# An encoder trunk in split fp32: the two parts of x pass the upper weights in one 512-column matmul, in separate PSUM banks

## The chip, the core and the metric

The kernel runs on one core of one Trainium2 chip. The metric is the time of one execution on the device in microseconds (us). The engines are named as in the profile: PE (matmul), PEld (loading of its stationary operand), ACT, DVE, POOL and SP, which issues the DMAs. Each engine works through its own instructions in program order and waits at semaphores for the others.

## What is computed

Two layers (DEPTH = 2) over 256 tokens of 1024 features, each of three parts: a feed-forward part (FFN), a part with three token mixers, and a second FFN. Every part ends in a layer norm.

```python
def swiglu(x, w_gate, w_up, w_down):
    return (jax.nn.silu(x @ w_gate) * (x @ w_up)) @ w_down
...
    for l in range(DEPTH):
        x = layer_norm(ALPHA * x + 0.5 * swiglu(x, ffn1_w_gate[l], ffn1_w_up[l], ffn1_w_down[l]),
                       ln_g[l, 0], ln_b[l, 0])
        proj = x @ w_in[l]
        u, gb, gc, h, q, k, v = jnp.split(proj, splits, axis=-1)
        y_a = pool_mixer(u, pool_w[l], pool_scale[l])
        y_b = gated_conv_mixer(gb, gc, h, conv_w[l])
        y_c = neighbourhood_attention(q, k, v, rpb[l])
        y = jnp.concatenate([y_a, y_b, y_c], axis=-1) @ w_out[l]
        x = layer_norm(ALPHA * x + y, ln_g[l, 1], ln_b[l, 1])
        x = layer_norm(ALPHA * x + 0.5 * swiglu(x, ffn2_w_gate[l], ffn2_w_up[l], ffn2_w_down[l]),
                       ln_g[l, 2], ln_b[l, 2])
```

The hidden width of an FFN is 2816 (22 chunks of 128). Attention has 8 heads of 64 features; a query sees all 4 grid rows and 16 of the 64 columns.

## The kernel before

**Numbers in two parts.** Every weight and every activation that meets a weight is kept as an upper part (`hi`, fp32r, an ACT cast) and a rest (`lo`, a DVE subtraction). A product is the sum of three: hi x hi, hi x lo, lo x hi; so every product is three matmuls.

**Weights.** 320 units of 128 x 1024 numbers (512 KB) come from memory in the order of `plan`. `load` (L182) issues the DMA on SP into `raw`, then the cast (L179) and the subtraction (L180). At most 12 units are live (`W_SLOTS` is 24 tiles); a unit's tiles are taken over when PE has read it for the last time.

**Order.** The schedule is written by hand. `Pacer` keeps a model clock: `step(us)` moves it on, runs the hooks that have come due (`at(delay, tag, fn)`) and emits the load of one more unit. `need(tag)` runs the hooks of a tag at once. So the order on every engine is that in which the program's lines run.

**Three kinds of product.** `x_stat` (L275, the first gate/up columns and v, u, gate of the mixers): x is stationary, the weights stream, 512 columns each. `w_stat` (L295): the weights are stationary, x streams, so that the result comes out transposed (features x tokens). One call computes 256 features for all 256 tokens: two halves (`ft`) of 128 features, 8 chunks of the contraction each, three matmuls of 256 columns per chunk; both halves lie in one PSUM bank of 512 columns. An FFN calls it for 9 pairs of hidden chunks, gate and up; a mixer part for q0, k0, q1, k1, gc and h. `r_stat` (L312): down and output projections, 512 columns, accumulated over all chunks in four banks (2 token halves x 2 feature halves).

**PSUM.** Eight banks in two pools of four: `mm` for everything that is soon read out, `acc` for the scores S of attention and for the four accumulators of `r_stat`. A new tile takes over the bank of the tile four allocations earlier in its pool, once that has been read out.

**Reading out.** A gate goes from its bank through ACT's silu (L392), an up by DVE with the gate (L397), then into hi and lo (L481, L482). q goes by ACT in mirrored pieces (L772), k and gc by ACT copies (L776, L788), h by a DVE product with gc (L794).

**The mixer part.** Its order after v, u and gate is: q0, k0, then attention of head group 0 by hooks while q1, k1 run; attention of group 1 while gc and h run. Attention is a chain: scores (L699, PE), bias and maximum (L708, L710, DVE), exponential (L713, ACT), normalisation (L723, L725, DVE), transposes (L734, PE), copies (L739, ACT), product with v (L748, PE), and its parts (L761 ACT, L762 DVE). The convolution (L675 to L681) follows h on DVE. Then comes the output projection (L804 on), over the chunks in the order 0, 1, 4, 5, 6, 7, 2, 3: the pool mixer's two chunks, attention's four, the convolution's two.

Of the kernel before, what the change touches and what calls it, by code (L numbers as in the profile page):

```python
# [63 lines left out]
MM256 = 0.1095  # L64
# [57 lines left out]
def encoder_kernel(  # L122
# [172 lines left out]
    def w_stat(ps, key, xT):  # L295

        for ft in range(2):
            c = slice(ft * P, (ft + 1) * P)
            for i in range(2):
                hi, lo = pc.get((*key, i))  # L300
                for j in range(4):
                    kc = i * 4 + j
                    o = ps[:, ft * SEQ : (ft + 1) * SEQ]
                    PE.matmul(o, hi[:, j, c], xT[0][:, kc, :], start=(kc == 0), stop=False)  # L304
                    PE.matmul(o, hi[:, j, c], xT[1][:, kc, :], start=False, stop=False)  # L305
                    PE.matmul(o, lo[:, j, c], xT[0][:, kc, :], start=False, stop=(kc == KC - 1))  # L306
# [93 lines left out]
    def ffn(key, xT, next_gb, stop, store=False):  # L400
        hts = {0: new_h(), 1: new_h()}

        def gated_transposed(t, gate, up):
            hf = gated(up, gate[0])

            def tr_():
                tr = bank().rearrange("p (a b) -> p a b", a=4)
                for j in range(4):
                    PE.transpose(tr[:, j, :], hf[:, j * P : (j + 1) * P], ident)
                ts = slice(t * P, (t + 1) * P)  # L410
                for q in range(2):
                    src = tr[:, 2 * q : 2 * q + 2, :]
                    ACT.copy(hts[q][:, 0, :, ts], src)
                    DVE.tensor_tensor(hts[q][:, 1, :, ts], src, f32(hts[q][:, 0, :, ts]), ALU.subtract)
# [55 lines left out]
        for p in range(2, NPAIR):  # L470
            if key[1] == 0 and p == 6:
                pc.at(0, "bias", bias_ahead)
            gate = bank()
            w_stat(gate, (*key, "g", p), xT)
            sg = silu(gate)
            pc.step(12 * MM256)
            up = bank()
            w_stat(up, (*key, "u", p), xT)
            hT = hts[p] = new_h()
            hf = gated(up, sg).rearrange("p (a b) -> p a b", a=2)  # L480
            ACT.copy(hT[:, 0], hf)  # L481
            DVE.tensor_tensor(hT[:, 1], hf, f32(hT[:, 0]), ALU.subtract)  # L482
            pc.step(12 * MM256)
            pc.need("h")

            for q in behind(p):
                for f in (2 * q, 2 * q + 1):
                    k = (*key, "d", f)
                    for t in range(NT):
                        for n in range(2):  # L490
                            if acc[t][n] is None:
                                acc[t][n] = bank("acc")
                            r_stat(acc[t][n], k, act(k), t, n, f == 0, False)
                        if t == 1:
# [103 lines left out]
    def mixers(l, xT, next_gb, stop):  # L598
# [11 lines left out]
        POOL.memset(U[:, :, PADL + SEQ :], 0.0)  # L610
        biases, rv1 = dict(ahead.pop("bias")), ahead.pop("rv")

        def pool_means():
# [15 lines left out]
            def product():  # L629
                ps = bank().rearrange("p (a b) -> p a b", a=2)  # L630
# [34 lines left out]

        def proj(name):
            ps = bank()
            w_stat(ps, (*key, name), xT)
            return ps.rearrange("p (a b) -> p a b", a=2)
# [13 lines left out]
        def attention(j, qT, kT, q):  # L683
# [59 lines left out]
            def weighted():  # L743
                po = bank()[:, 0:SEQ].rearrange("p (b r c) -> p b r c", b=2, r=ROWS)
# [21 lines left out]
        def qk(q):  # L766
            pq = proj(f"q{q}")
            qT = hp.tile([P, 2, 2, P], F32, tag="qk", bufs=4, name=nm("qT"))
            for j in range(2):
# [24 lines left out]
        DVE.tensor_tensor(z[:, :, 1 : SEQ + 1], p_, gc, ALU.mult)  # L794
# [64 lines left out]
```

## Time and profile before

| what | value |
|---|---|
| median of 3 runs | 964.16 us (964.05 to 966.96) |
| the profiled execution | 966.65 us, its span 964.9 us |
| granted PE clock, mean | 0.996 |
| weights' cast L179 / rest L180 | 321 each, 1045 / 1240 ns |
| 512-column matmuls, L316 to L318 and L291 to L293 | 3 x 416 and 3 x 192 |
| DMA | 178.95 MB, mean 185 GB/s |

The page's slices show how evenly PE is used (busy tenths in 40 slices, then the clock granted and the share of the DMA engines):

```profile
PE   7999999998999999999999999999999999999996
...
PEclk9999999999999999999999999999999999999998
DMA  8877685447543776565458766754664358666601
```

The first layer's mixer part lies at about 206 to 292 us of the span, the second's at 682 to 765 us; the rest but for the first 30 us are FFNs. A matmul's record begins when the one before is still in flight, so records overlap, and the pace of PE is read from the distance of two starts.

### The profile page before, as it was taken

The numbers are of one execution on the slowest core, as the hardware profiler recorded it, in microseconds if no ns is written. First come the engines' busy times: TensorE is split into PE (matmuls) and PEld (weight loads), VectorE is DVE, ScalarE is ACT, GpSimd is POOL, SyncE is SP. The second block draws the span as 40 slices with busy tenths as digits, with TensorE's granted clock in tenths as the row PEclk, the third lists the DMA queues.
The fourth block names the chain that finished last, engine by engine and source line by source line (L and its number), as shares of the span: only waits on it lengthen the run. The fifth ranks groups of instructions, "written<-read, shape, count | busy, mean of one in ns | idle before, by whom it ended". The sixth has DMA issues, their size and how long they took to land.

```text
span 964.9 us, 15250 instructions
## 1 busy us (share of the span) xinstructions
PE 946.9 (98%) x6201; PEld 861.3 (89%) x6201; DVE 572.1 (59%) x682; ACT 437.4 (45%) x585; POOL 58.6 (6%) x106
## 2 busy tenths in 40 slices
PE   7999999998999999999999999999999999999996
PEld 5999999988888999999888999998898889999995
DVE  5756364685678654544686445556766775454525
ACT  6545344344834544443354444444465454444420
POOL 4000100004100000000000001000050000000000
PEclk9999999999999999999999999999999999999998
DMA  8877685447543776565458766754664358666601
GB/s 285 286 238 248 162 244 181 145 150 218 158 131 132 242 238 189 182 197 175 131 176 257 222 189 172 223 178 145 193 216 126 122 188 273 182 179 189 190 23 43
DMA packets 129077, 178.95 MB, mean 185 GB/s; under 512 B 14752, under 2 KB 100848, under 8 KB 129008
## 3 DMA queue, kind: packets, MB, share of 16 engines
q1 hardware_dynamic: 129008, 177.99, 59.8%
q8 instruction: 48, 0.79, 0.3%
q14 instruction: 21, 0.17, 0.1%
HBM read 176.84 MB, written 1.13 MB: 184 GB/s over the span
## 4 chain that ended last, share of the span: by engine, by line
PE 89%; ACT 3%; DVE 3%; DMA 3%; issue 1%; SPq 0%; DVEq 0%; ACTq 0%
PE mm L304 15%; PE mm L305 15%; PE mm L306 15%; PE acc L316 10%; PE acc L317 10%; PE acc L318 10%; PE mm L293 4%; PE mm L291 4%; PE mm L292 4%; DVE wlo L180 2%; ACT whi L179 2%; ACT pz L713 1%; DMA raw<-in_w_in_dram 1%; PE mm L734 1%; DMA raw<-in_ffn_w_up_dram 1%; PE mm L269 1%
## 5 line engine op out<-in xcount | busy, mean ns | idle before, releaser
L180 DVE TENSOR_TENSOR wlo<-raw,whi 128x1024 fp32r<-128x1024 f32 (+1 forms) x321 | 392.2, 1240 | 302.6 <-ACT whi L179 299.3
L179 ACT CAST whi<-raw 128x1024 fp32r<-128x1024 f32 (+1 forms) x321 | 330.9, 1045 | 323.6 <-issue 111.0
L304 PE MATMUL mm<-xhi,whi 128*128 128x256 f32 x1344 | 382.3, 284 | 0.0
L305 PE MATMUL mm<-xlo,whi 128*128 128x256 f32 x1344 | 381.0, 283 | 0.0
L306 PE MATMUL mm<-xhi,wlo 128*128 128x256 f32 x1344 | 380.9, 283 | 0.0
L304 PEld LDWEIGHTS mm<-xhi,whi 128*128 128x128 f32 x1344 | 258.4, 192 | 2.8 <-issue 1.5
L305 PEld LDWEIGHTS mm<-xlo,whi 128*128 128x128 f32 x1344 | 258.5, 192 | 1.3
L306 PEld LDWEIGHTS mm<-xhi,wlo 128*128 128x128 f32 x1344 | 258.5, 192 | 0.0
L316 PE MATMUL acc<-whi,hT 128*128 128x512 f32 x352 | 137.9, 392 | 0.0
L317 PE MATMUL acc<-whi,hT 128*128 128x512 f32 x352 | 137.4, 390 | 0.0
L318 PE MATMUL acc<-wlo,hT 128*128 128x512 f32 x352 | 137.0, 389 | 0.0
L318 PEld LDWEIGHTS acc<-wlo,hT 128*128 128x128 f32 x352 | 66.1, 188 | 14.0
L316 PEld LDWEIGHTS acc<-whi,hT 128*128 128x128 f32 x352 | 66.2, 188 | 12.7
L317 PEld LDWEIGHTS acc<-whi,hT 128*128 128x128 f32 x352 | 66.2, 188 | 12.4
L291 PE MATMUL mm<-whi,xhi 128*128 128x512 f32 x192 | 77.0, 401 | 0.0
L293 PE MATMUL mm<-wlo,xhi 128*128 128x512 f32 x192 | 75.4, 393 | 0.2 <-DVE wlo L180 0.2
L292 PE MATMUL mm<-whi,xlo 128*128 128x512 f32 x192 | 75.4, 393 | 0.0
L481 ACT CAST hT<-hf 128x512 fp32r<-128x512 f32 x36 | 22.3, 620 | 75.2 <-DVE hf L397 75.2
L344 POOL TENSOR_TENSOR rs<-rs,half_t 128x1 f32<-128x1 f32 x12 | 11.7, 977 | 653.4 <-DVE rs L343 653.4
L293 PEld LDWEIGHTS mm<-wlo,xhi 128*128 128x128 f32 x192 | 36.3, 189 | 8.7 <-DVE wlo L180 1.1
L291 PEld LDWEIGHTS mm<-whi,xhi 128*128 128x128 f32 x192 | 36.4, 190 | 8.1 <-ACT whi L179 1.2
L292 PEld LDWEIGHTS mm<-whi,xlo 128*128 128x128 f32 x192 | 36.5, 190 | 7.1
(93 smaller groups left out, 535.9 us busy)
## 6 DMA issues: line engine op xcount, KB each, us to landing
raw<-in_ffn_w_up_dram SPq DMA_DIRECT2D x88, 512.0 KB, 4.8
raw<-in_ffn_w_down_dram SPq DMA_DIRECT2D x88, 512.0 KB, 4.2
raw<-in_ffn_w_gate_dram SPq DMA_DIRECT2D x87, 512.0 KB, 4.2
raw<-in_w_in_dram SPq DMA_DIRECT2D x40, 512.0 KB, 4.4
raw<-in_w_out_dram SPq DMA_DIRECT2D x16, 512.0 KB, 4.6
lng<-in_ln_g_dram SPq DMA_DIRECT2D x6, 512.0 KB, 4.8
lnb<-in_ln_b_dram SPq DMA_DIRECT2D x6, 512.0 KB, 6.1
rbias<-tab SPq DMA_DIRECT2D x16, 96.0 KB, 3.3
```

The source lines that it names most:

```text
L179: ACT.copy(hi, raw)
L180: DVE.tensor_tensor(lo, raw, f32(hi), ALU.subtract)
L291: PE.matmul(ps, xT[0][:, kc, ts], hi[:, j, :], start=(kc == 0), stop=False)
L292: PE.matmul(ps, xT[1][:, kc, ts], hi[:, j, :], start=False, stop=False)
L293: PE.matmul(ps, xT[0][:, kc, ts], lo[:, j, :], start=False, stop=(kc == KC - 1))
L304: PE.matmul(o, hi[:, j, c], xT[0][:, kc, :], start=(kc == 0), stop=False)
L305: PE.matmul(o, hi[:, j, c], xT[1][:, kc, :], start=False, stop=False)
L306: PE.matmul(o, lo[:, j, c], xT[0][:, kc, :], start=False, stop=(kc == KC - 1))
L316: PE.matmul(ps, act[0][:, ts], hi[:, n, :], start=first, stop=False)
L317: PE.matmul(ps, act[1][:, ts], hi[:, n, :], start=False, stop=False)
L318: PE.matmul(ps, act[0][:, ts], lo[:, n, :], start=False, stop=last)
L481: ACT.copy(hT[:, 0], hf)
```

## The change

1. x's two parts lie in one tile, per chunk of the contraction 256 columns of hi and 256 of lo side by side. In `w_stat` the stationary upper weights meet both parts in one matmul of 512 columns; the rest of the weights then meets the hi part, into the first 256 columns. Two matmuls per chunk take the place of three.
2. Each half of 128 features has a bank of its own. When a half is done, ACT copies columns 256 to 511 to SBUF (with the scale) and DVE adds columns 0 to 255. What followed (silu, product with the gate, mirrored copies of q, product with gc) reads the sum from SBUF, with one step more.
3. The banks of `mm` are thus used up twice as fast. The transposes of hidden chunks, the pool mixer's product, the transposes of the softmax, attention's product with v and the transposed constants take banks of `acc`.
4. All attention is emitted ahead of the output projection; `columns` (constants) moves from the first FFN to the first mixer part. The model clock counts 0.347 us per chunk.

```diff
     def new_xT():
-        hi = xp.tile([P, KC, SEQ], F32R, tag="xhi", name=nm("xhi"))
-        lo = xp.tile([P, KC, SEQ], F32R, tag="xlo", name=nm("xlo"))
-        return hi, lo
+        both = xp.tile([P, KC, 2, SEQ], F32R, tag="xT", name=nm("xT"))
+        return both[:, :, 0], both[:, :, 1], both.rearrange("p k i s -> p k (i s)")
...
-    def w_stat(ps, key, xT):
+    def w_stat(key, xT, out, scale=1.0):
+        ps = [bank() for _ in range(2)]
         for ft in range(2):
             c = slice(ft * P, (ft + 1) * P)
             for i in range(2):
                 hi, lo = pc.get((*key, i))
                 for j in range(4):
                     kc = i * 4 + j
-                    o = ps[:, ft * SEQ : (ft + 1) * SEQ]
-                    PE.matmul(o, hi[:, j, c], xT[0][:, kc, :], start=(kc == 0), stop=False)
-                    PE.matmul(o, hi[:, j, c], xT[1][:, kc, :], start=False, stop=False)
-                    PE.matmul(o, lo[:, j, c], xT[0][:, kc, :], start=False, stop=(kc == KC - 1))
+                    PE.matmul(
+                        ps[ft], hi[:, j, c], xT[2][:, kc], start=(kc == 0), stop=False, skip_group_check=True
+                    )
+                    PE.matmul(
+                        ps[ft][:, 0:SEQ], lo[:, j, c], xT[0][:, kc],
+                        start=False, stop=(kc == KC - 1), skip_group_check=True,
+                    )
                 if ft == 1:
                     pc.free((*key, i))
+                if i == 1:
+                    o = out[:, ft]
+                    ACT.activation(o, ps[ft][:, SEQ:], AF.Copy, scale=scale)
+                    DVE.scalar_tensor_tensor(o, ps[ft][:, 0:SEQ], scale, o, ALU.mult, ALU.add)
                 if ft == 0 or i == 0:
-                    pc.step(12 * MM256)
+                    pc.step(4 * MM768)
...
-            gate = bank()
-            w_stat(gate, (*key, "g", p), xT)
-            sg = silu(gate)
...
+            sg = tp.tile([P, 2, SEQ], F32, tag="t", name=nm("sg"))
+            w_stat((*key, "g", p), xT, sg)
+            ACT.activation(sg, sg, AF.Silu)
...
-            hf = gated(up, sg).rearrange("p (a b) -> p a b", a=2)
+            DVE.tensor_tensor(hf, hf, sg, ALU.mult)
...
-                    tr = bank().rearrange("p (a b) -> p a b", a=2)
+                    tr = bank("acc").rearrange("p (a b) -> p a b", a=2)
...
-                po = bank()[:, 0:SEQ].rearrange("p (b r c) -> p b r c", b=2, r=ROWS)
+                po = bank("acc")[:, 0:SEQ].rearrange("p (b r c) -> p b r c", b=2, r=ROWS)
...
-        DVE.tensor_tensor(z[:, :, 1 : SEQ + 1], p_, gc, ALU.mult)
+        DVE.tensor_tensor(z[:, :, 1 : SEQ + 1], h, gc, ALU.mult)
...
-        pc.need("ya")
-        pc.need("a0")
+        for tag in ("ya", "a0", "a1"):
+            pc.need(tag)
```

Two places in the order matter below. The first is PE at the end of the first layer's mixer part. Before, from the last product of attention (into the banks mm_2911, whose rows stand just ahead, and mm_2921) to the first matmuls of the output projection (four accumulators acc_...):

```order
L748 MATMUL mm_2921<-PT_2857,v_2101 64x256
L748 MATMUL mm_2921<-PT_2864,v_2101 64x256
L316 MATMUL acc_2936<-whi_2363,yT_2606 128x512
L317 MATMUL acc_2936<-whi_2363,yT_2606 128x512
L318 MATMUL acc_2936<-wlo_2364,yT_2606 128x512
L316 MATMUL acc_2940<-whi_2363,yT_2606 128x512
L317 MATMUL acc_2940<-whi_2363,yT_2606 128x512
L318 MATMUL acc_2940<-wlo_2364,yT_2606 128x512
L316 MATMUL acc_2944<-whi_2363,yT_2606 128x512
```

and now the same stretch (acc_2645 just ahead), with the semaphores for which a row waits in brackets:

```order
L753 MATMUL acc_2655<-PT_2597,v_1898 64x256
L753 MATMUL acc_2655<-PT_2604,v_1898 64x256
L324 MATMUL acc_2670<-whi_2155,yT_2360 128x512 [waits PE_49]
L325 MATMUL acc_2670<-whi_2155,yT_2360 128x512
L326 MATMUL acc_2670<-wlo_2156,yT_2360 128x512
L324 MATMUL acc_2674<-whi_2155,yT_2360 128x512 [waits PE_49]
L325 MATMUL acc_2674<-whi_2155,yT_2360 128x512
L326 MATMUL acc_2674<-wlo_2156,yT_2360 128x512
L324 MATMUL acc_2678<-whi_2155,yT_2360 128x512 [waits DVE_49,PE_49]
L325 MATMUL acc_2678<-whi_2155,yT_2360 128x512
L326 MATMUL acc_2678<-wlo_2156,yT_2360 128x512
L324 MATMUL acc_2682<-whi_2155,yT_2360 128x512 [waits DVE_49,PE_49]
```

The order of the matmuls is the same; the product with v is now in `acc`, and the third and fourth accumulators wait for DVE, which empties acc_2645 and acc_2655. On DVE those are the rows of L767, behind h's second half (L316), z and the convolution:

```order
L180 TENSOR_TENSOR wlo_2616<-raw_2614,whi_2615 128x1024
L316 SCALAR_TENSOR_TENSOR h_2557<-mm_2559,h_2557 128x256
L799 TENSOR_TENSOR z_2630<-h_2557,gc_2450 128x2x256
L680 TENSOR_SCALAR cs_2634<-z_2630,cw 128x256
L682 SCALAR_TENSOR_TENSOR cs_2634<-z_2630,cw,cs_2634 128x256 x2
L680 TENSOR_SCALAR cs_2634<-z_2630,cw 128x256
L682 SCALAR_TENSOR_TENSOR cs_2634<-z_2630,cw,cs_2634 128x256 x2
L683 TENSOR_TENSOR cs_2634<-cs_2634,GB_1900 128x512
L686 TENSOR_TENSOR yT_2642<-cs_2634,yT_2642 128x512
L767 TENSOR_TENSOR yT_2650<-acc_2645,yT_2650 128x4x32 x2
L767 TENSOR_TENSOR yT_2650<-acc_2655,yT_2650 128x4x32 x2
```

Before, DVE has the same rows there but for the one of L316. The second place is DVE ahead of the normalisation of head group 1 (reciprocal and scaling of the softmax). Before:

```order
L710 TENSOR_REDUCE mx_2742<-Sb_2740 128x2
L180 TENSOR_TENSOR wlo_2777<-raw_2775,whi_2776 128x1024
L723 RECIPROCAL sm_2717<-sm_2717 128x2
L725 TENSOR_SCALAR pz_592<-pz_592,sm_2717 128x4x40 x2
L723 RECIPROCAL sm_2724<-sm_2724 128x2
```

and now:

```order
L715 TENSOR_REDUCE mx_2496<-Sb_2494 128x2
L316 SCALAR_TENSOR_TENSOR gc_2450<-mm_2451,gc_2450 128x256
L180 TENSOR_TENSOR wlo_2525<-raw_2523,whi_2524 128x1024
L316 SCALAR_TENSOR_TENSOR gc_2450<-mm_2452,gc_2450 128x256
L728 RECIPROCAL sm_2471<-sm_2471 128x2
L730 TENSOR_SCALAR pz_564<-pz_564,sm_2471 128x4x40 x2
```

The evictions of gc's two halves now stand around the weight split (on ACT their copies stand around its cast in the same way); head group 0 has the halves of q1 there.

More of the change, by code (lines that the diff above doesn't have):

```diff
@@ L63 @@
 MM512 = 0.218
-MM256 = 0.1095
+MM768 = 0.347
 class Pacer:
@@ L406, in tr_ @@
             def tr_():
-                tr = bank().rearrange("p (a b) -> p a b", a=4)
+                tr = bank("acc").rearrange("p (a b) -> p a b", a=4)
                 for j in range(4):
@@ L472, in ffn @@
                 pc.at(0, "bias", bias_ahead)
-            gate = bank()
-            w_stat(gate, (*key, "g", p), xT)
-            sg = silu(gate)
-            pc.step(12 * MM256)
-            up = bank()
-            w_stat(up, (*key, "u", p), xT)
+            sg = tp.tile([P, 2, SEQ], F32, tag="t", name=nm("sg"))
+            w_stat((*key, "g", p), xT, sg)
+            ACT.activation(sg, sg, AF.Silu)
+            pc.step(4 * MM768)
+            hf = tp.tile([P, 2, SEQ], F32, tag="t", name=nm("hf"))
+            w_stat((*key, "u", p), xT, hf, 0.5)
             hT = hts[p] = new_h()
-            hf = gated(up, sg).rearrange("p (a b) -> p a b", a=2)
+            DVE.tensor_tensor(hf, hf, sg, ALU.mult)
             ACT.copy(hT[:, 0], hf)
             DVE.tensor_tensor(hT[:, 1], hf, f32(hT[:, 0]), ALU.subtract)
-            pc.step(12 * MM256)
+            pc.step(4 * MM768)
             pc.need("h")
@@ L546, in columns @@
         def columns():
-            trp = bank()[:, 0:16]
+            trp = bank("acc")[:, 0:16]
             PE.transpose(trp, rows, ident[0:16, 0:16])
             DVE.tensor_copy(cw, trp)
-        pc.at(30, "cw", columns)
+        consts["columns"] = columns
         tab = ap_.tile([P, 7 * TABW], F32, tag="a", name="tab")
@@ L610, in mixers @@
         POOL.memset(U[:, :, PADL + SEQ :], 0.0)
+        if l == 0:
+            pc.at(POOL_AT - 4, "cw", consts["columns"])
         biases, rv1 = dict(ahead.pop("bias")), ahead.pop("rv")
@@ L629, in product @@
             def product():
-                ps = bank().rearrange("p (a b) -> p a b", a=2)
+                ps = bank("acc").rearrange("p (a b) -> p a b", a=2)
                 for j in range(2):
@@ L664, in mixers @@
             pc.step(6 * MM512)
[L666 to L669, printed above, removed]
         def conv_mixer(z):
@@ L766, in qk @@
         def qk(q):
-            pq = proj(f"q{q}")
+            pq = tp.tile([P, 2, SEQ], F32, tag="t", name=nm("q"))
+            w_stat((*key, f"q{q}"), xT, pq, HD ** -0.5)
             qT = hp.tile([P, 2, 2, P], F32, tag="qk", bufs=4, name=nm("qT"))
@@ L771, in qk @@
                     src = mirrored(pq[:, j, :].rearrange("p (r c) -> p r c", c=GRID)[:, :, b * QB : (b + 1) * QB])
-                    ACT.mul(qT[:, j, b, :].rearrange("p (r c) -> p r c", c=QB), src, HD ** -0.5)
-            pc.step(12 * MM256)
-            pk = proj(f"k{q}")
+                    ACT.copy(qT[:, j, b, :].rearrange("p (r c) -> p r c", c=QB), src)
+            pc.step(4 * MM768)
             kT = hp.tile([P, 2, SEQ], F32, tag="qk", bufs=4, name=nm("kT"))
-            ACT.copy(kT, pk)
+            w_stat((*key, f"k{q}"), xT, kT)
             first = attention(0, qT, kT, q)
@@ L780, in qk @@
             pc.at(A_S + A_STEP, f"a{q}", second)
-            pc.step(12 * MM256)
+            pc.step(4 * MM768)
         qk(0)
@@ L785, in mixers @@
         qk(1)
-        p_ = proj("gc")
         gc = ap_.tile([P, 2, SEQ], F32, tag="a", name=nm("gc"))
-        ACT.copy(gc, p_)
-        pc.step(12 * MM256)
-        p_ = proj("h")
+        w_stat((*key, "gc"), xT, gc)
+        pc.step(4 * MM768)
+        h = tp.tile([P, 2, SEQ], F32, tag="t", name=nm("h"))
+        w_stat((*key, "h"), xT, h)
         z = ap_.tile([P, 2, SEQ + 2], F32, tag="a", name=nm("z"))
@@ L793, in mixers @@
         POOL.memset(z[:, :, SEQ + 1 :], 0.0)
-        DVE.tensor_tensor(z[:, :, 1 : SEQ + 1], p_, gc, ALU.mult)
+        DVE.tensor_tensor(z[:, :, 1 : SEQ + 1], h, gc, ALU.mult)
         conv_mixer(z)
-        pc.step(12 * MM256)
+        pc.step(4 * MM768)
         acc = [[None, None], [None, None]]
```

1 line of the change is left out of this document (removed).

## The prediction

> **What bounds the kernel now.** I read the page first (busy shares, chain), then the PE timeline for the pace of single matmuls, then windows for that pace over long stretches. From the page:
>
> ```profile
> PE 946.9 (98%) x6201; PEld 861.3 (89%) x6201; DVE 572.1 (59%) x682; ACT 437.4 (45%) x585; POOL 58.6 (6%) x106
> ...
> PE 89%; ACT 3%; DVE 3%; DMA 3%; issue 1%; SPq 0%; DVEq 0%; ACTq 0%
> ...
> L304 PE MATMUL mm<-xhi,whi 128*128 128x256 f32 x1344 | 382.3, 284 | 0.0
> ```
>
> PE is on the chain for 89% of the span, and 3 x 1344 of its 6201 matmuls are the 256-column ones of `w_stat`. Their mean of 284 ns is no pace, since they overlap; the pace is the distance of two starts. Where the 256-column matmuls end and the 512-column ones of `r_stat` begin, the timeline of PE has:
>
> ```profile
> 101.18 0.28 PE L306 MATMUL mm<-xhi,wlo 128*128 128x256 f32 x1
> 101.30 0.40 PE L316 MATMUL acc<-whi,hT 128*128 128x512 f32 x1
> 101.54 0.40 PE L317 MATMUL acc<-whi,hT 128*128 128x512 f32 x1
> 101.77 0.39 PE L318 MATMUL acc<-wlo,hT 128*128 128x512 f32 x1
> ```
>
> A 256-column matmul takes 0.12 us also when a 512 follows; a 512 takes 0.23. Two windows, one inside a `w_stat` run and one inside an `r_stat` run, give the third digit (stretch, its length, then each engine's busy time with the records that touch it, the granted clock, DMA share, GB/s):
>
> ```profile
> 158.00:180.00 22.00, 22.00 (x185) 22.00 (x185) 9.87 (x9) 9.12 (x11) 0.00 (x0) 1.00 0.65 193
> 184.00:193.00 9.00, 9.00 (x41) 7.45 (x40) 6.35 (x11) 2.11 (x2) 1.00 (x1) 1.00 0.26 83
> ```
>
> A record of 0.28 us touches a window for 2.3 paces more than its start, one of 0.39 for 1.7, so there are some 183 starts in 22 us, **0.120 us** each, and 39.6 starts in 9 us, **0.227 us** each. PE has no gap in either; DVE and ACT are busy for less than half of the first. Twice the columns cost 0.107 us more, not 0.120 more: each matmul carries some 0.013 us that doesn't depend on its columns.
>
> **What the change saves.** Per weight block `w_stat` issued three matmuls of 256 (0.360 us); now it issues one of 512 and one of 256, 0.227 + 0.120 = 0.347 us. The columns are the same, one fixed part is gone: 0.013 us x 1344 = **-17.5 us**. The alternation of the two sizes is in no row of before; the first 512 after a 256 above took up to 0.24, which would leave 0.360 - 0.240 - 0.120 = 0 by these two digits, and a pace of 0.340 would give -27. I take the sum of the two steady paces, as the long windows are nearest, and count -16 to -19 as its usual spread.
>
> The Trainium skill, page "TensorE: Matmul & The Clock Gate", section "Back-to-back issue gap", puts the fixed part of a warm matmul at about 2.5 ns; by it the saving would be an estimated 1344 x 2.5 ns = 3.4 us. The two windows disagree with it here, and the measurement decides.
>
> **What the eviction adds.** The old code read each bank once, 512 columns on one engine. Now each half (128 features) has an ACT copy and a DVE add of 256 columns out of PSUM. The nearest rows by shape:
>
> ```profile
> L658 ACT COPY U<-mm 128x256 f32<-128x256 f32 x4 | 1.5, 371 | 2.5 <-PE mm L657 2.5
> L414 DVE TENSOR_TENSOR hT<-mm,hT 128x256 fp32r<-128x256 f32 x16 | 6.7, 423 | 3.7 <-ACT hT L413 3.5
> ```
>
> 84 projections have 168 halves; 168 x 0.37 = 62 us on ACT and 168 x 0.42 = 71 us on DVE, less what they replace. In the FFN parts I cost it at nothing: four halves add 1.5 us of ACT and 1.7 us of DVE to a stretch in which PE has 4 x 8 x 0.347 = 11.1 us of them and 24 x 0.227 = 5.4 us of `r_stat`, and a bank comes round only three halves (8.3 us) later. The thinnest cover is the end of an FFN, where the last hidden block is needed soon:
>
> ```profile
> L481 ACT CAST hT<-hf 128x512 fp32r<-128x512 f32 x36 | 22.3, 620 | 75.2 <-DVE hf L397 75.2
> L482 DVE TENSOR_TENSOR hT<-hf,hT 128x512 fp32r<-128x512 f32 x36 | 24.9, 693 | 24.7 <-ACT hT L481 24.7
> ```
>
> Eviction (0.37 + 0.42), product (like L482, 0.69), cast (0.62) and subtraction (0.69) make 2.8 us, with a weight split in between up to 4.0; its first use comes 18 matmuls of `r_stat` later, 4.1 us. If it isn't covered, it costs below 1 us in each of four parts. The joined x tile changes no wait: the casts and transposes around it keep their order. The transposes of hidden blocks move to `acc`, which has no other users then. But PE waits for DVE ahead of such a transpose today already in two of four parts (L409, row below), so that what 12 blocks before it save (12 x 0.013) is lost: +0.3 us.
>
> **The mixers, softmax.** Here covers are thin. Ahead of the transposes of the softmax (L734) PE waits already, four times, up to 0.6 us (who waited for whom: us in total, times, longest):
>
> ```profile
> PE mm L734 <- DVE pz L725: 1.4, 4, 0.6
> PEld mm L409 <- DVE hf L397: 0.9, 2, 0.5
> ```
>
> (The second row is that of the +0.3 above.) Layer 0, second group of heads; the timeline of PE, then of ACT and DVE:
>
> ```profile
> 266.05 0.28 PE L306 MATMUL mm<-xhi,wlo 128*128 128x256 f32 x1
> 266.58 0.45 PE L734 MATMUL mm<-ident,pz 128*128 128x128 f32 x2 [0.26 <-DVE pz L725]
> 263.73 1.04 ACT L179 CAST whi<-raw 128x1024 fp32r<-128x1024 f32 x1
> 264.80 1.23 DVE L180 TENSOR_TENSOR wlo<-raw,whi 128x1024 fp32r<-128x1024 f32 x1 [1.94 <-ACT whi L179]
> 265.94 0.16 DVE L723 RECIPROCAL sm<-sm 128x2 f32<-128x2 f32 x1
> 266.13 0.52 DVE L725 TENSOR_SCALAR pz<-pz,sm 128x160 f32<-128x160 f32 x2
> ```
>
> The normalisation stands behind a weight split on DVE, that one behind its cast on ACT. In the new order an eviction (0.37) stands on ACT ahead of the cast, and one on DVE (0.42) between split and reciprocal: up to 0.79 us later, while PE arrives 20 x 0.013 = 0.26 us earlier. Operations of one engine overlap by some 0.1 us, so 0.8 to 1.05 us of new wait; I take 0.9 at each of four places, **+3.6 us** (from 0.3 each, if the exponentials end earlier, to 1.6 each).
>
> **The mixers, output projection.** This is the largest price. The last product of attention (before L748, now L753) went to `mm` banks; now it goes to two of the four `acc` banks that the output projection needs. Its third accumulator waits until DVE has taken that product out. DVE does so behind the whole convolution, today as well:
>
> ```profile
> 271.55 1.23 DVE L180 TENSOR_TENSOR wlo<-raw,whi 128x1024 fp32r<-128x1024 f32 x1 [1.89 <-ACT whi L179]
> 272.69 0.69 DVE L794 TENSOR_TENSOR z<-mm,gc 128x512 f32<-128x512 f32 x1
> ...
> 278.27 0.28 DVE L762 TENSOR_TENSOR yT<-mm,yT 128x128 fp32r<-128x128 f32 x1
> 278.89 0.49 DVE L762 TENSOR_TENSOR yT<-mm,yT 128x128 fp32r<-128x128 f32 x2 [0.33 <-ACT yT L761]
> ```
>
> while PE goes on at once:
>
> ```profile
> 271.71 0.28 PE L306 MATMUL mm<-xhi,wlo 128*128 128x256 f32 x1
> 271.92 1.95 PE L748 MATMUL mm<-PT,v 128*64 128x256 f32 x16
> 273.80 0.50 PE L316 MATMUL acc<-whi,yT 128*128 128x512 f32 x1
> ...
> 275.31 0.39 PE L316 MATMUL acc<-whi,yT 128*128 128x512 f32 x1
> ```
>
> Counted from the last matmul of `h` (271.71): the third accumulator starts at 275.31, +3.6 us. The second subtraction, which empties the first bank, starts at 278.89 and takes 0.28: +7.46. In the new order the add of h's second half (0.42) and a split that stands some 0.1 us later come ahead of z, so +8.0. PE waits 8.0 - 3.6 = 4.4 us in each layer: **+8.9 us**. Queued behind the waiting matmul on PE are the rest of the projection and so the layer norm, and nothing else is due, so all of it shows.
>
> An idle PE then loses its clock. The one gap of before that is near, and the windows after it:
>
> ```profile
> 222.48 0.28 PE L306 MATMUL mm<-xhi,wlo 128*128 128x256 f32 x1
> 225.22 0.66 PE L657 MATMUL mm<-ident,un 128*128 128x128 f32 x4 [2.47 <-ACT un L652]
> 226.00:228.00 2.00, 2.00 (x12) 2.00 (x11) 1.56 (x2) 0.45 (x2) 1.41 (x1) 0.50 0.66 111
> 228.00:230.00 2.00, 2.00 (x14) 2.00 (x14) 0.00 (x0) 0.00 (x0) 1.84 (x3) 0.68 0.86 256
> 699.27 0.66 PE L657 MATMUL mm<-ident,un 128*128 128x128 f32 x4 [0.97 <-ACT un L652]
> 699.00:701.00 2.00, 1.73 (x15) 1.74 (x16) 1.78 (x2) 1.45 (x3) 0.41 (x1) 1.00 0.89 268
> ```
>
> After 2.5 us idle the clock was 0.50 until about 229.2 (half of a window that reads 0.68 on the whole), some 3.3 us at half pace, 1.6 us lost; after 1.0 us it stayed at 1.00. In a gap of 4.4 us part of such a stretch falls into the gap itself: if it ends 6.5 us after the idleness began, as here (222.8 to 229.2), 2 us at half pace are left, 1 us lost. Between 0 and 1.6 I take 1.2, twice: **+2.4 us**.
>
> The same page of the Trainium skill, section "Part 1: The HAM clock gate", wants at least one whole idle window of about 3.4 us, free-running, ahead of half clock. A gap of 4.4 us holds a whole window by chance in about three of ten cases, which would cut the 2.4 us to an estimated 0.7; but here 2.5 us were enough.
>
> **Sum** against the profiled execution (966.65 us, span 964.9): -17.5 + 0.3 + 3.6 + 8.9 + 2.4 = -2.3 us. That execution is 2.5 us above the median of the runs, so I apply it to the median: 964.16 - 2.3 = **961.9 us**.
>
> **Rivals.** (1) The accumulator doesn't wait, because it gets banks that ACT has long emptied. For it: the first two accumulators do. Against it: four banks for ten tiles, two of them just written. Time: -17.5 + 0.3 + 3.6 = -13.6, 950.6 us. Chance 0.09. (2) Slower: at the four softmax places the cast between the two evictions on ACT waits for its transfer, and the in-order engine holds back the second eviction, then DVE, then PE.
>
> ```profile
> ACT whi L179 <- DMA raw<-in_w_in_dram: 7.9, 8, 1.8
> ```
>
> Such waits last up to 1.8 us; at all four places that is +7.2, 969.1 us. It decides from 1.3 us each (4 x 1.3 - 2.3 = 2.9). Against it: none of the eight stands at these places today. Chance 0.07. (3) Slower, the change doesn't do what it says: PE keeps to 0.360 us for the new pair, because each matmul's fixed part grows with the mixing. Then 964.16 + 15.2 = 979.4 us; with a fixed part of only 2.5 ns (0.0025 x 1344 = 3.4 us saved) 976.0. This second time is the Trainium skill's rule above. The paces where sizes meet speak against both: 0.12 and 0.23. Chance 0.04 together.
>
> **How the numbers follow.** My forecast has 0.80. Its spread is about 3 us either way (stalls 3.9 to 5.0 each, clock 0 to 3.2, softmax 1.2 to 6.4, saving 16 to 19), so 957.0 to 966.0 keeps nearly all of it; the rivals lie outside. About 0.3% (2.9 us) is what a measurement of this kernel tells from no change: faster means below 961.3. From the forecast 0.33 falls there, 0.45 within, 0.02 above; with rival 1 faster is 0.42, rival 2 gives 0.02 to within and 0.05 to slower, rival 3 slower: 0.42, 0.47, 0.11.
>
> **What would show it.** Right: PE count near 4857, starts of L304 and L307 0.347 us apart as a pair in the FFN parts; a wait of PE at L324 of some 4.4 us in each layer, put down to DVE yT L767, and a clock below 1.00 behind it; waits of about 1 to 1.5 us ahead of L739. Wrong: pairs at 0.36, no wait at L324, or PE idle in the FFN parts behind evictions (L316).

## The result, and the profile after

| kernel | median | range | runs |
|---|---|---|---|
| before (run beside it) | 965.47 us | 964.05 to 966.96 | 4 |
| changed | 974.69 us | 972.74 to 975.60 | 4 |

The ratio is 1.0093, 95% interval 1.0067 to 1.0118: the change makes the kernel 9 us **slower**. The prediction said 961.9 us. The profiled execution took 975.6 us, its span is 973.8 us against 964.9 before (+8.9, where the prediction had -2.3), its mean clock 0.989 against 0.996.

The page of the changed kernel, busy times, chain by engine, and the two groups that take the place of L304 to L306 (instructions, busy us, mean ns of one, idle time before):

```profile
PE 943.6 (97%) x4857; PEld 791.2 (81%) x4857; DVE 632.8 (65%) x850; ACT 493.3 (51%) x747; POOL 59.7 (6%) x106
...
PE 84%; DVE 5%; ACT 5%; DMA 4%; issue 1%; SPq 0%; DVEq 0%; ACTq 0%
...
L304 PE MATMUL mm<-xT,whi 128*128 128x512 f32 x1344 | 478.1, 399 | 0.0
L307 PE MATMUL mm<-xT,wlo 128*128 128x256 f32 x1344 | 377.3, 281 | 0.0
```

1344 matmuls are gone (6201 to 4857), and PE's busy time fell by only 3.3 us. DVE and ACT grew by 61 and 56 us. PE's share of the chain fell from 89% to 84%: more of the end is set by waits.

**Where PE waits** (who for whom, us in total, times, longest):

```profile
PE acc L324 <- DVE yT L767: 8.7, 2, 4.4
PE acc L739 <- DVE pz L730: 4.5, 4, 1.3
```

The first row didn't exist before; the second was 1.4 in all. No row puts PE behind the evictions of an FFN (L316). The stall on the timeline of PE, then of DVE, layer 0:

```profile
273.15 0.40 PE L326 MATMUL acc<-wlo,yT 128*128 128x512 f32 x1
277.92 0.77 PE L324 MATMUL acc<-whi,yT 128*128 128x512 f32 x1 [4.37 <-DVE yT L767]
278.48 0.63 PE L325 MATMUL acc<-whi,yT 128*128 128x512 f32 x1
...
283.17 0.63 PE L324 MATMUL acc<-whi,yT 128*128 128x512 f32 x1
283.60 0.52 PE L325 MATMUL acc<-whi,yT 128*128 128x512 f32 x1
...
272.06 0.35 DVE L680 TENSOR_SCALAR cs<-z,cw 128x256 f32<-128x256 f32 x1
...
276.25 0.69 DVE L686 TENSOR_TENSOR yT<-cs,yT 128x512 fp32r<-128x512 f32 x1 [0.68 <-ACT yT L685]
276.86 0.28 DVE L767 TENSOR_TENSOR yT<-acc,yT 128x128 fp32r<-128x128 f32 x1
277.48 0.49 DVE L767 TENSOR_TENSOR yT<-acc,yT 128x128 fp32r<-128x128 f32 x2 [0.33 <-ACT yT L766]
```

The third accumulator (277.92) starts when DVE has emptied the first bank, and DVE comes to that only after the whole convolution (L680 to L686). Less the matmul itself (0.227), the stall is 277.92 - 273.15 - 0.23 = 4.54 us, and 4.51 in layer 1. Behind it a 512-column matmul takes 0.43 us instead of 0.23 until 283.6. The windows (length, engines' busy time, granted clock, DMA share, GB/s) say why:

```profile
278.00:284.00 6.00, 6.00 (x15) 4.76 (x16) 2.74 (x3) 2.25 (x3) 0.00 (x0) 0.51 0.34 90
284.00:290.00 6.00, 6.00 (x28) 4.97 (x27) 1.23 (x1) 1.05 (x1) 0.00 (x0) 1.00 0.51 150
```

**The pace of the new pairs**, inside an FFN:

```profile
150.09 0.40 PE L304 MATMUL mm<-xT,whi 128*128 128x512 f32 x1
150.32 0.28 PE L307 MATMUL mm<-xT,wlo 128*128 128x256 f32 x1
150.44 0.40 PE L304 MATMUL mm<-xT,whi 128*128 128x512 f32 x1
150.68 0.28 PE L307 MATMUL mm<-xT,wlo 128*128 128x256 f32 x1
150.80 0.40 PE L304 MATMUL mm<-xT,whi 128*128 128x512 f32 x1
151.03 0.28 PE L307 MATMUL mm<-xT,wlo 128*128 128x256 f32 x1
151.15 0.40 PE L304 MATMUL mm<-xT,whi 128*128 128x512 f32 x1
```

Three pairs take 1.06 us, 0.353 each, not 0.347. To the nanosecond the pairs of a run repeat 350, 361, 349. The 512 behind a 256 takes mostly 0.236 us, the 256 behind it 0.117.

**The softmax**, layer 0, second group; PE, DVE, ACT:

```profile
263.12 0.28 PE L307 MATMUL mm<-xT,wlo 128*128 128x256 f32 x1
264.72 2.55 PE L739 MATMUL acc<-ident,pz 128*128 128x128 f32 x16 [1.32 <-DVE pz L730]
...
262.60 1.22 DVE L180 TENSOR_TENSOR wlo<-raw,whi 128x1024 fp32r<-128x1024 f32 x1 [0.52 <-ACT whi L179]
263.74 0.42 DVE L316 SCALAR_TENSOR_TENSOR gc<-mm,gc 128x256 f32<-128x256 f32 x1
264.08 0.15 DVE L728 RECIPROCAL sm<-sm 128x2 f32<-128x2 f32 x1
...
261.27 0.36 ACT L315 ACTIVATE gc<-mm 128x256 f32<-128x256 f32 x1
261.53 1.04 ACT L179 CAST whi<-raw 128x1024 fp32r<-128x1024 f32 x1
```

The eviction's copy stands ahead of the cast on ACT, its add between split and reciprocal on DVE. PE's distance from the last projection matmul to the transposes is 1.60 us here, 0.53 before (266.05 to 266.58).

For the experiments the trace of each kernel is summed the same way: distances from one PE start to the next, in us, inside the projections (`w_stat`), inside the down and output projections (`r_stat`, stalls included), and from the matmul ahead to the first transpose of the softmax (four places).

| kernel | `w_stat` | `r_stat` | to L739 | rest | span |
|---|---|---|---|---|---|
| before | 480.3 | 275.2 | 2.7 | 206.7 | 964.9 |
| changed | 469.7 | 290.8 | 5.6 | 207.7 | 973.8 |
| e1 product's bank undone | 469.5 | 276.1 | 5.7 | 206.7 | 957.9 |
| e2 read out first | 469.7 | 276.1 | 5.7 | 206.9 | 958.3 |
| e3 three of 256 | 479.0 | 288.0 | 5.3 | 207.2 | 979.4 |
| e4 groups of four | 466.2 | 288.8 | 4.8 | 207.9 | 967.8 |
| e5 wait filled | 469.8 | 285.7 | 4.7 | 206.8 | 966.9 |
| e6 groups of eight | 462.7 | 287.5 | 6.6 | 207.3 | 964.0 |
| e11 = e1 + e6 | 462.7 | 275.2 | 6.2 | 208.3 | 952.4 |
| e12 thinner evictions | 469.9 | 276.2 | 2.9 | 205.9 | 954.8 |

(e5's `r_stat` has its added matmuls in it, 18 in each layer, 9.6 us with the waits around them.)

### The profile page after: what moved, and what is told of

Read it like the earlier page. It is cut to its first block, busy times and chain, and to the rows that moved or that the text cites. A ratio compares the mean times of both kernels' runs of the same rounds, so it can differ in the third digit from the quotient of the medians.

```text
span 973.8 us, 12906 instructions
## 1 busy us (share of the span) xinstructions
PE 943.6 (97%) x4857; PEld 791.2 (81%) x4857; DVE 632.8 (65%) x850; ACT 493.3 (51%) x747; POOL 59.7 (6%) x106
## 4 chain that ended last, share of the span: by engine, by line
PE 84%; DVE 5%; ACT 5%; DMA 4%; issue 1%; SPq 0%; DVEq 0%; ACTq 0%
PE mm L304 29%; PE mm L307 15%; PE acc L324 10%; PE acc L326 10%; PE acc L325 10%; PE mm L292 3%; PE mm L290 3%; PE mm L291 3%; DVE wlo L180 3%; ACT whi L179 2%; DMA raw<-in_ffn_w_up_dram 2%; DMA raw<-in_w_in_dram 1%; PE mm L268 1%; ACT pz L718 1%; DMA raw<-in_ffn_w_gate_dram 1%
## 5 line engine op out<-in xcount | busy, mean ns | idle before, releaser
L304 PE MATMUL mm<-xT,whi 128*128 128x512 f32 x1344 | 478.1, 399 | 0.0
L307 PE MATMUL mm<-xT,wlo 128*128 128x256 f32 x1344 | 377.3, 281 | 0.0
L304 PEld LDWEIGHTS mm<-xT,whi 128*128 128x128 f32 x1344 | 252.5, 188 | 62.8 <-issue 1.5
L307 PEld LDWEIGHTS mm<-xT,wlo 128*128 128x128 f32 x1344 | 253.8, 189 | 1.4
L290 PE MATMUL mm<-whi,xT 128*128 128x512 f32 x192 | 77.0, 401 | 1.2 <-ACT whi L179 1.2
L326 PEld LDWEIGHTS acc<-wlo,hT 128*128 128x128 f32 x352 | 66.1, 188 | 14.7
L292 PE MATMUL mm<-wlo,xT 128*128 128x512 f32 x192 | 75.8, 395 | 0.5 <-DVE wlo L180 0.5
L291 PE MATMUL mm<-whi,xT 128*128 128x512 f32 x192 | 75.5, 393 | 0.0
L315 ACT ACTIVATE sg<-mm 128x256 f32<-128x256 f32 x72 | 27.5, 382 | 57.6 <-PE mm L307 57.6
L316 DVE SCALAR_TENSOR_TENSOR sg<-mm,sg 128x256 f32<-128x256 f32 x72 | 30.2, 420 | 25.5 <-ACT sg L315 25.5
L292 PEld LDWEIGHTS mm<-wlo,xT 128*128 128x128 f32 x192 | 36.5, 190 | 9.3 <-DVE wlo L180 1.7
L290 PEld LDWEIGHTS mm<-whi,xT 128*128 128x128 f32 x192 | 36.5, 190 | 9.0 <-ACT whi L179 1.9
L291 PEld LDWEIGHTS mm<-whi,xT 128*128 128x128 f32 x192 | 36.5, 190 | 7.2
```

The lines of the kernel that those rows point to most:

```text
L290: PE.matmul(ps, xT[0][:, kc, ts], hi[:, j, :], start=(kc == 0), stop=False)
L291: PE.matmul(ps, xT[1][:, kc, ts], hi[:, j, :], start=False, stop=False)
L292: PE.matmul(ps, xT[0][:, kc, ts], lo[:, j, :], start=False, stop=(kc == KC - 1))
L304: PE.matmul(ps[ft], hi[:, j, c], xT[2][:, kc], start=(kc == 0), stop=False, skip_group_check=True)
L307: PE.matmul(ps[ft][:, 0:SEQ], lo[:, j, c], xT[0][:, kc], start=False, stop=(kc == KC - 1), skip_group_check=True,)
L315: ACT.activation(o, ps[ft][:, SEQ:], AF.Copy, scale=scale)
```

## The experiments

The theory after the comparison: the stall with its half clock costs about 14.7 us, a pair saves 7 ns and not 13, and the softmax costs 3. Each is undone alone below. Times stand against the kernel before, run on the same chip (966.2 to 966.6 us as the median). The changed kernel's 974.69 us stood beside a before of 965.47, so differences from it are sure to about 1 us only.

**e1, the stall's bank.**

```diff
-                po = bank("acc")[:, 0:SEQ].rearrange("p (b r c) -> p b r c", b=2, r=ROWS)
+                po = bank()[:, 0:SEQ].rearrange("p (b r c) -> p b r c", b=2, r=ROWS)
```

> Only the last product of attention goes back from the four shared banks to the four of the projections. Theory: in each layer the output projection's third accumulator waits 4.4 us for DVE's readout behind the convolution, and the clock is at half for 5.7 us after it (2.8 us lost); both go: 2 x 7.3 = -14.7 us against the changed kernel, so about 960 us, with the PE wait at L324 gone. Rival: the loss sits in the added evictions, which hold up ACT and DVE in the mixers, and the wait is only where it shows; then another wait takes its place (at the weight splits behind it or at L739) and at most half comes back: 967 to 975 us.

Measured 959.09 us (957.05 to 960.51), ratio 0.9925 (0.9903 to 0.9946): 15.6 us below the changed kernel, and faster than before. PE passes from the second to the third accumulator without a wait:

```profile
271.99 0.40 PE L326 MATMUL acc<-wlo,yT 128*128 128x512 f32 x1
272.23 0.39 PE L324 MATMUL acc<-whi,yT 128*128 128x512 f32 x1
```

`r_stat` falls by 14.7 us, the other columns of the table by 1.0 or less. One bank choice turns the change from a gain into a loss; the rival, evictions as such, falls.

**e2, the same stall by order.**

```diff
+        pc.need("a1")
         conv_mixer(z)
```

> The banks stay as in the changed kernel; the last heads' readout is put ahead of the convolution on DVE. Theory (the bank waits for DVE's queue, not for the data): DVE begins that readout at about 272 instead of 276.9 us, so the third accumulator is free at about 273.0 to 273.5 and PE waits 0 to 0.5 us; clock stays at 1.00; about 960 to 962 us, less if the convolution's product (used last by the projection) stays hidden, which it should. Rival (the readout itself, with its alternation of ACT and DVE, is the wait): half of the stall stays, above 966 us.

Measured 959.40 us (957.35 to 960.10), ratio 0.9926 (0.9906 to 0.9946). With the same four shared banks, DVE now has z, readout, convolution:

```profile
270.47 0.69 DVE L799 TENSOR_TENSOR z<-h,gc 128x512 f32<-128x512 f32 x1
271.08 0.28 DVE L767 TENSOR_TENSOR yT<-acc,yT 128x128 fp32r<-128x128 f32 x1
...
272.72 0.34 DVE L680 TENSOR_SCALAR cs<-z,cw 128x256 f32<-128x256 f32 x1
```

So the bank alone isn't the cause, nor is the readout's own length: it is the readout's place behind 4.8 us of convolution (272.06 to 276.86 in the changed kernel) on an in-order engine.

**e3, the change without its merging.**

```diff
-                        ps[ft], hi[:, j, c], xT[2][:, kc], start=(kc == 0), stop=False, skip_group_check=True
+                        ps[ft][:, 0:SEQ], hi[:, j, c], xT[0][:, kc], start=(kc == 0), stop=False,
+                        skip_group_check=True,
+                    )
+                    PE.matmul(
+                        ps[ft][:, SEQ:], hi[:, j, c], xT[1][:, kc], start=(kc == 0), stop=(kc == KC - 1),
+                        skip_group_check=True,
...
```

Two sums are now open in one bank at a time, and what this kernel computes is not the full sum; the instructions are all there, and only their time is used.

> Banks, evictions and order as in the changed kernel, but each block again takes three matmuls of 256 columns, so this is the change without its merging. Theory: a merged pair takes 0.353 us against 0.360 for the three, so 1344 x 0.007 = +9.4 us on the changed kernel, 984 us. By the prediction's 0.347 it would be +17.5, 992 us; if merging saved nothing, 975 us. The matmul count is 6201.

Measured 981.37 us (981.04 to 982.73), ratio 1.0159 (1.0141 to 1.0178). That is +6.7, less than the 9.4 expected. In the profiled execution `w_stat` grows by 9.3 us (479.0 - 469.7), as the theory has it, but `r_stat` falls by 2.8: 1.9 of it because the half clock behind the stalls was shorter (see e5), 0.9 because the 512s behind steady 256s start faster than those behind an alternation (see e6). So merging is worth 9.3 us in the projections, not 17.5, and costs 0.9 us behind them. The other three executions of e3 have mean clocks (0.990 to 0.992) like those of the changed kernel (0.989 to 0.994) and are still only about 7 us above it; this last 1 to 2 us is not explained.

**e4 and e6, the pace of the pairs.** e4 issues the four 512s of a unit and then its four 256s; e6 all eight 512s of a half and then its eight 256s (the diff is e6's):

```diff
+            units = [pc.get((*key, i)) for i in range(2)]
+            for kc in range(KC):
+                PE.matmul(
+                    ps[ft], units[kc // 4][0][:, kc % 4, c], xT[2][:, kc], start=(kc == 0), stop=False,
...
+            pc.step(4 * MM768)
+            for kc in range(KC):
+                PE.matmul(
+                    ps[ft][:, 0:SEQ], units[kc // 4][1][:, kc % 4, c], xT[0][:, kc],
...
```

> In each weight unit the four 512-column matmuls go first and then the four of 256, instead of taking turns. Theory: a 512 takes 0.236 us only behind a 256 and 0.227 behind a 512; a 256 takes 0.117 behind a 512 and 0.120 behind a 256. Then a unit takes 0.236 + 3 x 0.227 + 0.117 + 3 x 0.120 = 1.394 instead of 1.412 us, 336 units: -6.0 us, about 968.7 us. Rival: the 512 of these projections takes 0.236 whatever stands ahead of it (its columns come from two halves of the x tile), then no gain, or +3 us: 975 to 978 us.

> In each half projection all eight 512-column matmuls go first, then all eight of 256. Theory A (a 512 is slow while PE catches up from the 256s, some four or five matmuls long, as in the runs of the output projection: 233, 236, 229, 233, 231, then 227 ns): eight 512s take 234 + 234 + 231 + 231 + 231 + 3 x 227 = 1842 ns and eight 256s 8 x 118.5 = 948, so 2790 instead of 8 x 353.7 = 2830, 168 halves: about -6.7 us on the changed kernel, 968 us, with the sixth to eighth at 227. Theory B (a 512 of these projections takes 234 ns anyway): the sixth to eighth stand at 234 too, -1.7 us, 973 us. Weight units come free later by half a unit, which may cost a wait.

e4: 969.10 us (967.02 to 970.99), ratio 1.0028 (1.0016 to 1.0041). The time is near what was expected, but not for the reason given: the 512s of a run of four take 234, 234, 229, 231 ns (medians), so "only the first is slow" is wrong, and `w_stat` fell by 3.4 us where 6.0 were forecast; the rest of its gain lies in `r_stat` (-2.0) and in smaller waits. e6: 965.36 us (962.89 to 967.80), ratio 0.9990 (0.9976 to 1.0003). Its eight 512s, then the first of `r_stat` on the timeline:

```profile
148.72 2.00 PE L302 MATMUL mm<-xT,whi 128*128 128x512 f32 x8
150.57 1.12 PE L308 MATMUL mm<-xT,wlo 128*128 128x256 f32 x8
151.52 0.40 PE L325 MATMUL acc<-whi,hT 128*128 128x512 f32 x1
```

Over all 168 halves the medians by place in the run are 233, 236, 228, 232, 231, 227, 227, 227 ns, which is theory A; theory B (234 throughout) falls. The 512s of `r_stat` begin in the same way here and in before. So behind a run of 256s the first five 512s are slow, in both kinds of product, and an alternation never leaves that stretch. Behind an alternation the stretch is longer: in the changed kernel and in e1 the first ten 512s of `r_stat` take 224 to 241 ns (medians by place) before they come to 227, and without stalls that makes `r_stat` 276.1 us (e1) instead of 275.2 (e11). `w_stat` fell by 6.9 us (6.7 expected). The other 2.4 us of the gain lie elsewhere: `r_stat` -3.3 (2.0 of it a shorter half clock, 0.9 this faster start), waits at the transposes +0.9.

**e5, the clock alone.**

```diff
+                if k == keys[0] and t == 0:
+                    idle = bank()
+                    for m in range(18):
+                        PE.matmul(
+                            idle, act(k)[0][:, 0:P], pc.get(k)[0][:, 0, :], start=(m == 0), stop=(m == 17)
+                        )
```

> The changed kernel with 18 matmuls of 512 columns (4.1 us, result never read) put on PE ahead of the output projection's third accumulator, so that PE is busy through most of its wait. Theory (idleness takes the clock): the third accumulator starts as late as before, but the matmuls after it run at 0.227 us at once; the 13 at 0.427 us cost 2.7 us in each layer, so -5 to -5.6 us against the changed kernel, about 969 us. Rival (the slow stretch comes from something else, such as transfers or the readout beside it): the 13 slow matmuls stay, 974 to 975 us.

Measured 968.83 us (968.26 to 970.33), ratio 1.0030 (1.0020 to 1.0040): 5.9 below the changed kernel. PE's timeline, then the window that read 0.51:

```profile
273.29 4.25 PE L824 MATMUL mm<-whi,yT 128*128 128x512 f32 x18
277.83 0.47 PE L324 MATMUL acc<-whi,yT 128*128 128x512 f32 x1 [0.30 <-DVE yT L767]
```

```profile
278.00:284.00 6.00, 6.00 (x27) 4.71 (x27) 3.51 (x4) 3.24 (x4) 0.00 (x0) 1.00 0.34 96
```

The third accumulator starts as late as ever (277.83), but the clock in the same window is 1.00 instead of 0.51. Idleness of PE, not the transfers or the readout, takes the clock, and matmuls whose result nobody reads buy back 5 to 6 us.

How long half clock lasts is seen in windows set to its edges; on either side of each the granted clock is 1.00. The changed kernel's two stretches:

```profile
277.02:283.85 6.83, 5.93 (x14) 4.76 (x15) 3.36 (x6) 2.69 (x5) 0.00 (x0) 0.50 0.27 78
754.89:761.71 6.82, 5.73 (x14) 4.50 (x15) 3.56 (x7) 2.69 (x5) 0.00 (x0) 0.50 0.26 77
```

and those of e3, where PE was idle for 4.33 us ahead of each:

```profile
280.59:284.00 3.41, 3.29 (x8) 2.64 (x9) 1.70 (x3) 1.99 (x3) 0.00 (x0) 0.50 0.00 0
758.45:765.28 6.83, 4.62 (x11) 3.70 (x12) 3.94 (x7) 3.36 (x7) 0.00 (x0) 0.50 0.13 19
```

Between 100 and 900 us of the spans the kept traces have 14 such stretches, seven of 3.41 us and seven of 6.83. Equal gaps bring either one (e3, and e4 and e6 too), so the gap's length doesn't set it. What costs time is the part in which PE works (the first number behind the length), and half of it is lost: 5.8 us for the two stretches of the changed kernel, 4.0 in e3, 4.5 in e4, 3.8 in e6.

**e12, the softmax.** On top of e1:

```diff
+                    thin = key[2] in ("q1", "gc")
+                    if not (thin and ft == 0):
+                        ACT.activation(o, ps[ft][:, SEQ:], AF.Copy, scale=scale)
+                    if thin and ft == 0:
+                        DVE.tensor_scalar(o, ps[ft][:, 0:SEQ], scale, None, ALU.mult)
+                    elif not thin:
+                        DVE.scalar_tensor_tensor(o, ps[ft][:, 0:SEQ], scale, o, ALU.mult, ALU.add)
```

> e1, but in the two projections that run beside the softmax (q of the second heads, gc) each half is read out by one engine: the first half by DVE alone, without the part of the lower x and without ACT's copy, the second by ACT alone, without the sum of DVE; so these two projections lack one part each. Theory (prediction's softmax term: a copy of 0.37 us on ACT ahead of the cast, an add of 0.42 us on DVE between split and normalisation): cast, split and normalisation come some 0.3 + 0.4 us earlier at each of four places, so the distance from the last projection matmul to L739 goes from 1.41 to about 0.7 us, the sum from 5.65 to 2.7 to 3.0 us, and the time from 959.1 to about 956.3 us. Rival (the exponentials or the split's transfer set the normalisation): the sum stays at 5 us or more and the time at 959 us.

Measured 956.46 us (955.95 to 956.88), ratio 0.9901 (0.9885 to 0.9918). The distances to the transposes (L744 in this kernel) sum to 2.85 us instead of 5.65; PE's waits:

```profile
PE acc L744 <- DVE pz L735: 1.7, 4, 0.7
```

That is the wait of before (1.4). The added wait is the evictions' two places in the queues, as the prediction had it.

**e7 to e10, normalisation first.** On e1, the normalisation is emitted one step earlier:

```diff
-A_NORM = 3.6
-A_TR = 2.2
+A_NORM = 2.7
+A_TR = 3.5
```

> The last product of attention in the projections' banks (as in e1) and the softmax's normalisation emitted one step earlier, ahead of the weight split and the second eviction on DVE; the transposes stay where they were. Theory (the added waits at L739 are DVE's queue, as predicted): the exponentials end some 2.5 us before DVE reaches the normalisation, so all of the wait at L739 (5.6 us in four places, start to start) goes, against e1: about 953.5 to 954.5 us. Rival (the split that now stands behind makes weights late for PE): a wait on wlo takes its place, 957 to 960 us.

> e7 with the pool mixer's product in the projections' banks too. In e7 a transpose at L739 waited up to 3.7 us for ACT's readout of that product, since the four shared banks are handed round in order and the fourth transpose got its bank. Theory: with that bank gone nothing else holds L739, and the 7.1 us of e7 and the half clock behind it (3 us in the projections) go: about 953.5 to 954.5 us. Rival: the readout of the product still stands behind the same queue on ACT, and now a projection waits for its bank: 957 us or more.

e7: 963.10 us (960.88 to 964.98), ratio 0.9969 (0.9952 to 0.9986), slower than e1. The wait for DVE is gone and a longer one stands in its place; the row of PE's waits, then the timeline of PE and of ACT:

```profile
PE acc L739 <- ACT ya L646: 7.1, 2, 3.7
```

```profile
247.91 0.66 PE L739 MATMUL acc<-ident,pz 128*128 128x128 f32 x4 [3.35 <-ACT ya L646]
...
245.67 0.50 ACT L778 COPY qT<-q 128x128 f32<-128x128 f32 x2 [2.85 <-DVE q L316]
246.08 1.04 ACT L179 CAST whi<-raw 128x1024 fp32r<-128x1024 f32 x1
247.02 0.83 ACT L646 ACTIVATE ya<-acc,cw 128x256 f32<-128x256 f32 x2
```

Normalisation ahead of the eviction on DVE delays q's add; ACT's copies of q wait for that, and behind them stands the readout of the pool product, whose shared bank the fourth transpose gets. e9 takes that bank out of the ring (`bank()` for the pool product): 959.34 us (957.52 to 960.39), ratio 0.9917 (0.9895 to 0.9939), no better than e1; PE's waits:

```profile
PE mm L753 <- ACT PT L744: 2.9, 2, 1.7
...
PE acc L739 <- DVE pz L730: 1.4, 2, 0.7
```

PE waits less at the transposes and more at the product behind them. Neither theory held, and e7 came out above its rival's time too. e9's time is what its rival said, but PE waits there for the copied transposes and not for a bank. On two loaded in-order queues the wait moves.

> e7 with the grouping of e6. Theory: the gains add, e7's time less what e6 gains on the changed kernel (some 7 us): 947 us. Rival: weights that come free later collide with the later splits, and the two don't add: 950 to 955 us.

> e9 with the grouping of e6: its projections ran 6.9 us shorter there; if that adds to e9, about 947 us. Rival: with the grouping, the step boundaries shift, a wait at L739 for the normalisation stays (3 to 4 us in e8): 950 to 951 us.

With the grouping of e6, e8 measured 958.37 us (955.60 to 961.61), ratio 0.9909 (0.9883 to 0.9935), and e10 954.88 us (953.69 to 956.07), ratio 0.9877 (0.9860 to 0.9894). Both miss 947 and come out above their rivals' times. In e8 the wait for the pool product's bank is still there (5.2 us in two places), and in both the wait for the normalisation comes back with the grouping (e10, where L740 is the transpose):

```profile
PE acc L740 <- DVE pz L731: 4.1, 4, 1.6
```

**e11, the bank and the grouping together.** e1's bank and e6's grouping, nothing else:

> The last product of attention in the projections' banks (e1) and the grouping of e6, normalisation where the change has it. Theory (the two are independent: 14.7 us of wait and half clock, 6.9 us of matmul pace): 959.1 - 6.9 = about 952 us. Rival: units that come free later, with two more banks in use by attention, make PE wait in the mixers: 955 us or more.

Measured 953.49 us (950.96 to 954.23), ratio 0.9858 (0.9838 to 0.9878): 1.4% below before. It is the fastest of the kernels that compute the whole result. The two gains add in the sums: `w_stat` as in e6, `r_stat` without stalls. In the time it is 5.6 us below e1 and not 6.9; in the profiled execution `rest` took 1.6 us more. What is left of the change's price is the softmax:

```profile
PE acc L740 <- DVE pz L731: 5.0, 4, 1.7
```

## Why the prediction was wrong

It named every place at which time is won or lost and got two sizes wrong, both in the change's favour.

- **The saving, -17.5, was -9.3** (`w_stat` of e3 against the changed kernel; by the time it is less, 6.7). The failed step is "I take the sum of the two steady paces, as the long windows are nearest". The steady paces themselves are right (the second window has 39 starts, 0.227 us apart, though 41 records less 1.7 would make 0.229), but a steady pace says nothing of an alternation. The rows where the sizes meet, quoted beside it, had 0.24 for the first 512 and were set aside as an end of the range; by that one row, to two digits, there is no saving at all. A pair is 0.353 us, midway between 0.347 and 0.360: rival 3's mechanism (the fixed part grows with the mixing) was half right, for about half of the 13 ns. By the Trainium skill's fixed part of 2.5 ns (page "TensorE: Matmul & The Clock Gate", section "Back-to-back issue gap"), weighed there, the saving would have been an estimated 3.4 us. The measured 9.3 lie between this and 17.5. The term is 8.2 us of the 11.2 between forecast and profile (-2.3 and +8.9).
- **The half clock, +2.4, was 5 to 6** (e5: 5.9 in the time, 5.1 in the sums; changed kernel less e1: 14.7 - 9.05 = 5.7; by the granted clock 5.8). The failed step is "if it ends 6.5 us after the idleness began, as here". It ended 10.3 and 10.1 us after. In before the clock was 0.50 from 225.85 to 229.26, for 3.41 us that began 0.6 us after PE was at work again; here it was 0.50 for 6.83 us twice, from 0.9 and 1.1 us before PE's new start, so that 5.9 and 5.7 us of it fell on work. The longer gap didn't shorten that part here. The Trainium skill, page "TensorE: Matmul & The Clock Gate", section "Part 1: The HAM clock gate", says of the way back that full clock comes after at least one busy window of some 3.4 us, free-running, so an estimated 3.4 to 6.8 us after the work begins. The ends in before (4.0 us after PE's new start) and here (5.9 and 5.7) lie in that; one in e3 (3.3) and one in e6 (2.8) lie below it, and there the measurement decides. The prediction weighed only the page's other half, the idle window. Some of the size is chance: with the same stalls e3, e4 and e6 lost 3.8 to 4.5 us, which is still outside the 0 to 3.2 of the prediction.
- **The stall, +8.9, was 9.05** (4.54 + 4.51), at the instruction and the bank that were named, with the engine that was named as the one to empty it; e1 and e2 show its two conditions, the bank and the place behind the convolution.
- **The softmax, +3.6, was +2.9** (2.7 to 5.6 us over the four places), with the cause named; e12 confirms it.
- **The FFN evictions at nothing** holds: PE waits for none. The transposes of hidden blocks cost +0.2 (1.25 to 1.49 us ahead of L417) against +0.3.
- The rest comes to +0.4. Before loses 1.4 us more in `w_stat` than e3 with the same matmuls, as its clock falls to 0.61 (225 to 229 us) and e3's stays at 1.00. The matmuls of `x_stat`, which the change doesn't touch, took 132.7 us in this execution and 130.8 before (130.7 to 133.1 in the experiments): from 10.8 to 14.2 us, at the start of the program, the clock was 0.50 here and 1.00 in before. These two go with the clock of the two executions, and no run shows that the change causes them. The slower start of the 512s of `r_stat` behind the alternation, +0.9, does belong to it; the others are below 1 us each.
- Of the rivals, 1 (no wait) is what e1 does to the kernel: 959.1, not 950.6, by the same 8 us of saving. Rival 2's waits (ACT for a transfer of `w_in`) fell, from 7.9 to 4.4 us in all.

Open: why a 512 is slow for five matmuls after 256s, and why the pairs repeat 350, 361, 349. The runs show that it goes with the order of the sizes, and that 512s with the same kind of operands run at 227 ns from the sixth on; no run here looks inside PE. Open too: which of the two lengths of half clock a stall brings.

## What to carry over

Price a mix of instructions from several rows where the sizes meet, to the nanosecond, not from the two pure streams or from one rounded row, and group equal sizes if the order is free. Before tiles of a ring of buffers are shared with a later user, follow the last reader of each through its engine's whole queue: moving the reader or the tile was worth 15 us of 975 here, more than the optimisation itself. A stall of some 4 us on PE cost its length and then 1.4 to 3.0 us more at half clock here.

## What was unexpected

- Five 512-column matmuls behind a run of 256s take 233, 236, 228, 232 and 231 ns, then 227; behind an alternation it takes ten to come to 227. Eight of a kind in a row are enough to win back 6.9 us of 470.
- Half clock was granted for 3.41 or 6.83 us, never for another length between 100 and 900 us, and counted from PE's new start it ended after 2.8 to 6.1 us. 18 matmuls that nobody reads, put into the gap, prevent it.
- The gap's length alone doesn't decide whether the clock falls. Gaps of 2.5 us (before), 3.35 us (e7) and 1.6 us (e10) were followed by half clock, with transposes as PE's first work behind them; gaps of 1.7 us (changed kernel, 701.8) and 2.0 us (e6, 245.0), also ahead of transposes, were not.
- In e7 the half clock behind its 3.35 us of idleness made `w_stat` take 472.6 us against 469.5 in e1.
